# The triangular solves of the RWKV operands issued on VectorE in 30 parts a stage

## The chip, the core and the metric

The kernel runs on one core of a Trainium2 chip. The metric is the device time of one launch in microseconds. An execution's own time is its span, from the first to the last instruction of the program, and what lies around it.

## The reference, cut to what matters

One layer of a hybrid backbone, run over 256 context tokens and 2048 latent tokens, width 1024. One input projection feeds three token mixers: mLSTM (6 heads x 64), RWKV-7 (6 heads x 64) and RG-LRU (256 channels). Their outputs are gated, joined and go through one output projection. The mixers run in both directions.

The change touches RWKV-7. The reference is a scan over tokens, for each head and direction:

```python
def rwkv_step(S, inp):
    r, w, kh, b, kt, v = inp
    Sk = jnp.einsum('bhvk,bhk->bhv', S, kh)
    S = S * w[:, :, None, :] - Sk[..., None] * b[:, :, None, :] + v[..., None] * kt[:, :, None, :]
    return S, jnp.einsum('bhvk,bhk->bhv', S, r)
```

The kernel takes 64 tokens at a time (a chunk). Within a chunk the state products depend on one another through a strictly lower triangular 64x64 matrix, so each chunk needs the inverse of a unit triangular matrix. The kernel inverts its two 32x32 diagonal blocks by substitution and gets the third block by two matrix products.

## The kernel before, in words

The program is written by generators under a small planner (class `Flow`). The planner keeps a clock of its own, `F.now`, that grows with the estimated time of the matmuls it has issued. Each generator issues instructions and yields either a number of ns after which it may go on or an event. Of the generators that may go on the one with the lowest rank goes first; rank 9, the input projection (`projector`), is the filler and is taken when no other is ready, or when TensorE's estimated activity is low. TensorE executes in exactly this written order. The other engines' queues are put in order by a list scheduler from the written order and its own estimates. Every engine executes its queue in order.

The stages, with their times in the profile: inputs, gates and shifts (to about 640 us), `derive` (640 to 1056), `mlstm` (1056 to 1378), `chains` with the output projection (1378 to the end). The projection of 34 column groups runs beside the first three; its tiles are called `pp_` and the group (`pp_rz`, `pp_mo`, `pp_mz` are the last ones). Its very last group may only start after `mlstm`.

`derive` makes the RWKV operands. It has 54 blocks of 256 tokens and one direction, for a pair of heads each, in seven stages (one of 6 blocks, six of 8). `block()` does a block: four matmuls into `pw`, then ScalarE and VectorE in turn up to the tile `KB` (L955 to L972 are VectorE's seven or so instructions), and stores. A worker, one of three, then waits, multiplies `KB` into `pt` on TensorE (16 short matmul records), and copies its 32x32 parts into `DG` and `OF`. When a stage's blocks are through, `derive`'s own loop transposes `DG` into `W` (L1049), masks it on GpSimd (L1050, L1052) and solves: for j from 1 to 30 a product into `tmp` (L1058) and an addition into `W` (L1060), each of (31 - j) x j elements a partition. The two depend on each other and on the step before. `finish` waits, transposes `W` twice into `XT` (L1030, L1031), and starts `merge`: products `pY` and `pX` on TensorE and the store of `XT`. `W` has two buffers, and stage k takes its one when `finish` of stage k - 2 has read it. The last stage's `merge` ends `derive`; the memory of `derive` is then given to `mlstm`.

`mlstm` takes three head pairs. For each it first makes state changes for 18 chunks (`pk` are TensorE's transpositions, `pd` its products, L1261 the state recurrence on VectorE), then the outputs for 18 chunks with three workers (`pm`, `pn` on TensorE, L1301 to L1321 on VectorE). A head pair's states are made while the one before it gives its outputs.

Of the kernel before, what the change touches and what calls it, by code (L numbers as in the profile page):

```python
# [13 lines left out]
ALU = mybir.AluOpType  # L14
# [297 lines left out]
def side(X, ctx):  # L312
# [31 lines left out]
    with tc.tile_pool(name="dv", bufs=1, side="right") as dv:  # L344
        yield from derive(X, dv)
# [487 lines left out]
def derive(X, dv):  # L833
    nc, vec, hv, CH, F = X["nc"], X["vec"], X["hv"], X["CH"], X["F"]
# [62 lines left out]
    def merge(sid, XT, g, end):  # L897

        o = OF[sid]
        hs = [(slice(64 * h, 64 * h + 32), slice(64 * h + 32, 64 * h + 64)) for h in range(2)]  # L900
        yield 7000.0
        pY = X["ps"].tile([128, 16, 32], F32, tag="b", name=f"pY{sid}{g}")
        for l in range(16):
            for a, b in hs:
                F.mm(pY[b, l], o[a, g + l], XT[a, g + l, 32:64])
            if l % 4 == 3:
                yield 0.0
        for a, b in hs:
            nc.scalar.activation(o[b, g:g + 16], pY[b], AF.Copy, scale=-1.0)
        yield 3000.0  # L910
        pX = X["ps"].tile([128, 16, 32], F32, tag="b", name=f"pX{sid}{g}")
        for l in range(16):
            for a, b in hs:
                F.mm(pX[a, l], o[b, g + l], XT[b, g + l, 32:64])
            if l % 4 == 3:
                yield 0.0
        for a, b in hs:
            nc.scalar.activation(XT[a, g:g + 16, 32:64], pX[a], AF.Copy)
        end[0] -= 1
        if end[0]:  # L920
            return
        yield 1000.0
        for p, d, li, nch, lane in stages[sid]:
            for h in range(2):
                r = slice(64 * h, 64 * h + 64)
                nc.sync.dma_start(CH[p, d][r, li:li + nch, 64 + 192 * h:128 + 192 * h], XT[r, lane:lane + nch])
        F.fire(merged[sid])
# [94 lines left out]

    def finish(sid, W):

        yield 40500.0
        if sid and merged[sid - 1].t is None:
            yield merged[sid - 1]
        XT = dv.tile([128, 32, 64], F32, tag="XT", name=f"XT{sid}")
        with X["tc"].high_priority(offset=300):
            nc.vector.transpose(XT[:, :, 0:32].rearrange("p l t -> p t l"), W)  # L1030
            nc.vector.transpose(XT[:, :, 32:64].rearrange("p l s -> p s l"), W.rearrange("p t s -> p s t"))  # L1031
            for h in range(2):
                r = slice(64 * h + 32, 64 * h + 64)
                nc.vector.tensor_copy(XT[r, :, 32:64], XT[r, :, 0:32])
                nc.gpsimd.memset(XT[r, :, 0:32], 0.0)
        F.fire(read[sid])
        end = [2]
        for g in (0, 16):
            F.spawn(merge(sid, XT, g, end), 2)


    for sid, segs in enumerate(stages):
        if full[sid].t is None or full[sid].t > F.now:
            yield full[sid]
        if sid > 1 and read[sid - 2].t is None:
            yield read[sid - 2]
        W = dv.tile([128, 32, 32], F32, tag="W", name=f"W{sid}", bufs=2)
        with X["tc"].high_priority(offset=300):
            nc.vector.transpose(W, DG[sid].rearrange("p l t -> p t l"))  # L1049
        nc.gpsimd.affine_select(out=W, in_=W, pattern=[[1, 32], [-1, 32]], base=0, channel_multiplier=0,  # L1050
                                compare_op=ALU.is_gt, fill=0.0)
        nc.gpsimd.memset(W.rearrange("p a b -> p (a b)")[:, 0:1024:33], 1.0)  # L1052
        F.fire(taken[sid])
        tmp = dv.tile([128, 256], F32, tag="tmp", name=f"tmp{sid}")
        for j in range(1, 31):
            m = 31 - j
            tv = tmp[:, 0:m * j].rearrange("p (a b) -> p a b", a=m)
            nc.gpsimd.tensor_tensor(out=tv, in0=W[:, j + 1:32, j:j + 1].to_broadcast([128, m, j]),  # L1058
                                    in1=W[:, j:j + 1, 0:j].to_broadcast([128, m, j]), op=ALU.mult)
            nc.gpsimd.tensor_tensor(out=W[:, j + 1:32, 0:j], in0=W[:, j + 1:32, 0:j], in1=tv, op=ALU.add)  # L1060
        F.spawn(finish(sid, W), 2)
    yield merged[-1]

# [907 lines left out]
```

## Time and profile before

| | |
|---|---|
| median of 3 runs | 2062.82 us (2059.71 to 2068.17) |
| profiled execution | 2059.59 us, span 2057.9 us |
| TensorE (PE) busy | 1801.6 us, 88% |
| VectorE (DVE) busy | 1367.0 us, 66% |
| ScalarE (ACT) busy | 977.6 us, 48% |
| GpSimd (POOL) busy | 795.0 us, 39% |
| mean granted TensorE clock | 0.933 |

The shares are means over stages that differ much: GpSimd is busy four fifths of the time while it solves and hardly anywhere else before that. PEld is TensorE's load of weights, which overlaps PE. The rows below are in us except where they say ns; a row's last part is the engine's idle time just before such instructions and what ended it.

### The profile page before, as it was taken

The numbers are of one execution on the slowest core, as the hardware profiler recorded it, in microseconds if no ns is written. First come the engines' busy times: TensorE is split into PE (matmuls) and PEld (weight loads), VectorE is DVE, ScalarE is ACT, GpSimd is POOL, SyncE is SP. The second block draws the span as 40 slices with busy tenths as digits, with TensorE's granted clock in tenths as the row PEclk, the third lists the DMA queues.
The fourth block names the chain that finished last, engine by engine and source line by source line (L and its number), as shares of the span: only waits on it lengthen the run. The fifth ranks groups of instructions, "written<-read, shape, count | busy, mean of one in ns | idle before, by whom it ended". The sixth has DMA issues, their size and how long they took to land. (4 is left out here: it accounts for less than half of the span.)

```text
span 2057.9 us, 46221 instructions
## 1 busy us (share of the span) xinstructions
PE 1801.6 (88%) x16648; PEld 1201.0 (58%) x16778; DVE 1367.0 (66%) x3271; ACT 977.6 (48%) x2634; POOL 795.0 (39%) x1200
## 2 busy tenths in 40 slices
PE   5899999999999878788899798878778788999996
PEld 3555655656666556555566565555555556777774
DVE  3747366777643898998324766647885576777774
ACT  5732446565434667776242545542332233444442
POOL 0210011112110688888722444342653232444442
PEclk9899999999999988889999899989888999999997
DMA  7343344564548778887254666645986545576662
GB/s 284 118 142 90 126 123 133 153 168 148 132 127 247 215 207 223 225 214 176 80 154 135 188 171 170 171 118 154 292 268 193 164 136 149 163 196 203 197 190 72
DMA packets 353370, 350.60 MB, mean 170 GB/s; under 512 B 109554, under 2 KB 294978, under 8 KB 350728
## 3 DMA queue, kind: packets, MB, share of 16 engines
q1 hardware_dynamic: 353142, 347.65, 59.2%
q8 instruction: 133, 2.18, 0.5%
q14 instruction: 95, 0.78, 0.1%
HBM read 211.18 MB, written 136.37 MB: 169 GB/s over the span
## 5 line engine op out<-in xcount | busy, mean ns | idle before, releaser
L1635 POOL TENSOR_SCALAR sd<-cg,Dall 128x128 f32<-128x128 f32 x210 | 135.8, 654 | 267.1 <-DVE cg L1659 164.0
L1659 DVE SCALAR_TENSOR_TENSOR cg<-cq,Dall,sd 64x64 f32<-64x64 f32 x408 | 114.5, 281 | 46.4 <-PE cq L168 36.6
L1060 POOL TENSOR_TENSOR W<-W,tmp 128x30 f32<-128x30 f32 (+14 forms) x210 | 139.0, 662 | 16.1
L1058 POOL TENSOR_TENSOR tmp<-W 128x30 f32<-128x30 f32 (+14 forms) x210 | 133.0, 633 | 15.9
L168 PE MATMUL cq<-cg,bt 128*64 128x64 f32 x840 | 68.5, 246 | 49.7 <-DVE cg L1644 44.6
L1283 ACT ACTIVATE nb<-nb,aT 128x128 f32<-128x128 f32 x216 | 71.6, 393 | 82.5 <-DMA nb<-nm_d 72.4
L168 PE MATMUL cq<-cg 128*64 128x64 f32 x1728 | 92.9, 230 | 8.2 <-DVE cg L1659 8.2
L168 PEld LDWEIGHTS cq<-cg,bt 128*64 128x64 f32 x840 | 44.1, 142 | 84.9 <-DVE cg L1644 54.8
L168 PE MATMUL ga<-cg 64*64 64x128 f32 (+1 forms) x864 | 76.9, 270 | 16.9 <-DMA cg<-ch 16.9
L1630 ACT ACTIVATE q<-cq 128x64 f32<-128x64 f32 x216 | 45.5, 223 | 95.7 <-PE cq L168 92.3
L1592 DVE TENSOR_TENSOR cg<-gb,rmask 64x256 f32<-64x256 f32 x108 | 44.7, 413 | 66.3 <-PE gb L168 61.1
L168 PEld LDWEIGHTS cq<-cg 128*64 128x64 f32 x1728 | 72.9, 141 | 24.3 <-issue 9.5
L168 PE MATMUL pz<-owhi,zhi 128*128 128x512 f32 x180 | 82.1, 456 | 4.5 <-ACT zhi L1822 4.5
L1598 ACT ACTIVATE bt<-ga 128x256 f32<-128x256 f32 x108 | 41.3, 383 | 87.0 <-DVE G L1595 83.4
L168 PE MATMUL pt<-KB 64*64 64x64 f32 x864 | 41.9, 244 | 45.7 <-DVE KB L972 45.6
L1284 POOL TENSOR_SCALAR_AFFINE_SELECT nb<-nb 128x256 f32<-128x256 f32 x108 | 44.8, 421 | 93.0 <-ACT nb L1283 63.6
L168 PE MATMUL gb<-cg 64*64 64x128 f32 (+1 forms) x864 | 75.7, 270 | 0.9 <-DMA cg<-ch 0.9
L168 PE MATMUL pz<-owhi,zlo 128*128 128x512 f32 x180 | 73.5, 409 | 3.3 <-DVE zlo L1823 3.3
L168 PE MATMUL pz<-owlo,zhi 128*128 128x512 f32 x180 | 72.9, 405 | 0.0
L168 PEld LDWEIGHTS ga<-cg 64*64 64x64 f32 x864 | 48.2, 142 | 41.9 <-issue 27.9
L168 PE MATMUL cq<-q,cg 128*64 128x64 f32 x864 | 59.4, 236 | 9.9 <-ACT q L1630 9.9
L168 PE MATMUL pp_v<-hhi,whi_v 128*128 128x512 f32 (+1 forms) x120 | 67.4, 562 | 0.3 <-ACT whi_v L514 0.3
(511 smaller groups left out, 6180.0 us busy)
## 6 DMA issues: line engine op xcount, KB each, us to landing
cg<-ch SPq DMA_DIRECT2D x216, 192.0 KB
wa<-wa SPq DMA_DIRECT2D x54, 256.0 KB
z<-z SPq DMA_DIRECT2D x27, 512.0 KB
ch<-KB SPq DMA_DIRECT2D x108, 128.0 KB
ch<-KB SPq DMA_DIRECT2D x54, 256.0 KB
nb<-nm_d SPq DMA_DIRECT2D x108, 128.0 KB
lr<-L SPq DMA_DIRECT2D x16, 768.0 KB
lL<-lr SPq DMA_DIRECT2D x16, 768.0 KB
```

The source lines that it names most:

```text
L168: self.nc.tensor.matmul(out, lhsT, rhs, start=start, stop=stop, **kw)
L1058: nc.gpsimd.tensor_tensor(out=tv, in0=W[:, j + 1:32, j:j + 1].to_broadcast([128, m, j]), in1=W[:, j:j + 1, 0:j].to_broadcast([128, m, j]), ...
L1060: nc.gpsimd.tensor_tensor(out=W[:, j + 1:32, 0:j], in0=W[:, j + 1:32, 0:j], in1=tv, op=ALU.add)
L1283: nc.scalar.activation(nb[:, d, j], nb[:, d, j], AF.Exp, bias=aT[:, c, d, 2 * p + j:2 * p + j + 1])
L1284: nc.gpsimd.affine_select(out=nb[:, d], in_=nb[:, d], pattern=[[0, 2], [1 - 2 * d, 128]], base=0, channel_multiplier=-1 + 2 * d, compare_o ...
L1592: nc.vector.tensor_tensor(out=cg[o, :, RK[h]], in0=src[o], in1=mask[o, d].rearrange("p a c -> p (a c)")[:, None].to_broadcast([64, 2, 128] ...
L1598: nc.scalar.activation(bt, ga[:, 1], AF.Copy)
L1630: nc.scalar.activation(q, qk, AF.Copy, scale=-1.0)
L1635: nc.gpsimd.tensor_scalar(sd, cg.rearrange("p (n c) -> p n c", c=64)[:, 0::9], Dk, None, op0=ALU.mult)
L1659: nc.vector.scalar_tensor_tensor(out=nxt[h][b], in0=ps[b], scalar=Dk[b], in1=sd[b, 1 - h], op0=ALU.mult, op1=ALU.add)
```

## The change

The 60 instructions of a stage's solve are issued on VectorE instead of GpSimd. After each of the 30 steps the loop yields for 800 ns of the planner's clock, so that blocks and filler are written in between; before, the 60 instructions were written in one piece. `finish` waits for 6 us of that clock instead of 40.5.

```diff
     def finish(sid, W):
 
-        yield 40500.0
+        yield 6000.0
         if sid and merged[sid - 1].t is None:
             yield merged[sid - 1]
         XT = dv.tile([128, 32, 64], F32, tag="XT", name=f"XT{sid}")
...
         for j in range(1, 31):
             m = 31 - j
             tv = tmp[:, 0:m * j].rearrange("p (a b) -> p a b", a=m)
-            nc.gpsimd.tensor_tensor(out=tv, in0=W[:, j + 1:32, j:j + 1].to_broadcast([128, m, j]),
+            nc.vector.tensor_tensor(out=tv, in0=W[:, j + 1:32, j:j + 1].to_broadcast([128, m, j]),
                                     in1=W[:, j:j + 1, 0:j].to_broadcast([128, m, j]), op=ALU.mult)
-            nc.gpsimd.tensor_tensor(out=W[:, j + 1:32, 0:j], in0=W[:, j + 1:32, 0:j], in1=tv, op=ALU.add)
+            nc.vector.tensor_tensor(out=W[:, j + 1:32, 0:j], in0=W[:, j + 1:32, 0:j], in1=tv, op=ALU.add)
+
+            yield 800.0
         F.spawn(finish(sid, W), 2)
```

VectorE's queue in `derive`, at one block of the second stage (`KB_0_7681`; `cs` and `E` are its decay factors, `z` its loaded operands). Before:

```order
L959 TENSOR_SCALAR KB_0_7681_6152<-KB_0_7681_6152,rab 128x4x64
L955 TENSOR_SCALAR cs_0_7681_6155<-KB_0_7681_6152 128x256
L965 TENSOR_TENSOR KB_0_7681_6152<-KB_0_7681_6152,z_0_768_5887 128x4x128
L956 SCALAR_TENSOR_TENSOR cs_0_7681_6155<-sm,cs_0_7681_6155 128x256
L967 TENSOR_TENSOR KB_0_7681_6152<-E_5316,z_0_768_5887 128x4x64
L969 TENSOR_TENSOR KB_0_7681_6152<-E_5316,z_0_768_5887 128x4x64
L972 TENSOR_TENSOR KB_0_7681_6152<-cs_0_7681_6155,KB_0_7681_6152 128x4x128
L955 TENSOR_SCALAR cs_0_10240_6259<-KB_0_10240_6256 128x256
L959 TENSOR_SCALAR KB_0_10240_6256<-KB_0_10240_6256,rab 128x4x64
```

The block's seven instructions follow each other, and the next block's come right behind them.

The same block now (`W` and `tmp` are those of the first stage's solve):

```order
L959 TENSOR_SCALAR KB_0_7681_6108<-KB_0_7681_6108,rab 128x4x64
L972 TENSOR_TENSOR KB_0_7680_6068<-cs_0_7680_6071,KB_0_7680_6068 128x4x128
L955 TENSOR_SCALAR cs_0_7681_6111<-KB_0_7681_6108 128x256
L1058 TENSOR_TENSOR tmp_5941<-W_5937 128x168
L965 TENSOR_TENSOR KB_0_7681_6108<-KB_0_7681_6108,z_0_768_5887 128x4x128
L956 SCALAR_TENSOR_TENSOR cs_0_7681_6111<-sm,cs_0_7681_6111 128x256
L1060 TENSOR_TENSOR W_5937<-W_5937,tmp_5941 128x24x7
L1058 TENSOR_TENSOR tmp_5941<-W_5937 128x184
L967 TENSOR_TENSOR KB_0_7681_6108<-E_5316,z_0_768_5887 128x4x64
L969 TENSOR_TENSOR KB_0_7681_6108<-E_5316,z_0_768_5887 128x4x64
L1060 TENSOR_TENSOR W_5937<-W_5937,tmp_5941 128x23x8
L972 TENSOR_TENSOR KB_0_7681_6108<-cs_0_7681_6111,KB_0_7681_6108 128x4x128
```

Between the seven instructions of the block stand instructions of the solve, and where no block is ready they follow each other.

TensorE's queue near the end of `mlstm`, in the outputs of the third head pair (`pm` and `pn` are its products, `pp_mo` is projection). Before:

```order
L168 MATMUL pm_14544<-kq_14278 128x128
L168 MATMUL pm_14544<-dl_12404,kq_14278 128x130
L168 MATMUL pm_14550<-kq_14278 128x128
L168 MATMUL pm_14550<-dl_12404,kq_14278 128x130
L168 MATMUL pm_14555<-kq_14278 128x128
L168 MATMUL pm_14555<-dl_12404,kq_14278 128x130
L168 MATMUL pn_14560<-v_10445,nb_14384 64x65 x8
L168 MATMUL pp_mo_3_14490<-hhi,whi_mo_13783 128x512
L168 MATMUL pp_mo_3_14490<-hhi,wlo_mo_13784 128x512
L168 LDWEIGHTS w_mo_13785
L168 MATMUL pp_mo_3_14490<-hlo,w_mo_13785 128x512
L168 MATMUL pp_mo_3_14490<-hhi,whi_mo_13783 128x512
```

Pieces of six projection matmuls stand between the products.

The same part now:

```order
L168 MATMUL pm_14580<-kq_14361 128x128
L168 MATMUL pm_14580<-dl_12810,kq_14361 128x130
L168 MATMUL pm_14585<-kq_14361 128x128
L168 MATMUL pm_14585<-dl_12810,kq_14361 128x130
L175 MATMUL hT_14590<-ident,H 128x128 x4
L168 MATMUL pm_14599<-kq_14361 128x128
L168 MATMUL pm_14599<-dl_12810,kq_14361 128x130
L168 MATMUL pm_14604<-kq_14361 128x128
L168 MATMUL pm_14604<-dl_12810,kq_14361 128x130
L168 MATMUL pn_14609<-v_10847,nb_14455 64x65 x8
L168 MATMUL pn_14625<-v_10849,nb_14476 64x65 x8
L168 MATMUL pn_14641<-v_10851,nb_14497 64x65 x8
```

The projection that stood between the products isn't there any more. It stands in `derive`: TensorE's order holds 1284 projection matmuls between the first `pw` and the first `pk`, 990 before. In the first half of `mlstm` as much of it stands in the same places, and from the first matmul of the chains on TensorE's order is the same as before.

## Rows read from the trace of the kernel before

**Rows 1.** Windows of five stages: us, busy us of each engine, PEclk, DMA, GB/s.

```profile
680.00:975.00 295.00, 239.42 (x2754) 165.41 (x2784) 272.36 (x373) 210.81 (x652) 252.90 (x364) 0.85 0.79 207
975.00:1056.00 81.00, 72.32 (x790) 47.53 (x797) 22.30 (x26) 21.69 (x38) 46.28 (x101) 0.94 0.37 97
1056.00:1205.00 149.00, 135.50 (x1028) 87.55 (x1043) 80.40 (x296) 64.17 (x203) 59.10 (x142) 0.94 0.61 168
1205.00:1292.00 87.00, 72.97 (x695) 49.88 (x702) 56.45 (x229) 44.75 (x137) 43.19 (x98) 0.94 0.63 171
1292.00:1378.00 86.00, 72.44 (x637) 47.86 (x643) 50.43 (x187) 42.53 (x100) 34.10 (x79) 0.96 0.48 138
```

**Rows 2.** Groups of GpSimd, 680 to 1026 us: busy us, mean ns, idle before.

```profile
L1060 POOL TENSOR_TENSOR W<-W,tmp 128x30 f32<-128x30 f32 (+14 forms) x210 | 139.0, 662 | 16.1
L1058 POOL TENSOR_TENSOR tmp<-W 128x30 f32<-128x30 f32 (+14 forms) x210 | 133.0, 633 | 15.9
```

**Rows 3.** Waits of GpSimd, 684 to 1026 us: us, times, longest.

```profile
POOL W L1050 <- DVE W L1049: 7.3, 5, 2.4
```

**Rows 4.** Single lines and tiles: ns min/median/max, first and last start, forms.

```profile
L1058 POOL TENSOR_TENSOR tmp<-W x210: 237/610/1117, 683.6 to 1024.5; 128x30 f32<-128x30 f32 x7, 128x84 f32<-128x84 f32 x7, 128x130 f32<-128x130 f32 x7, 128x168 f32<-128x168 f32 x7
...
L1031 DVE STREAM_TRANSPOSE XT<-W x7: 2062/2092/2223, 731.7 to 1026.9; 128x1024 f32<-128x1024 f32 x7
...
L168 PE MATMUL pt<-KB x864: 218/218/366, 652.3 to 969.1; 64*64 64x64 f32 x173
...
L175 PE MATMUL pk<-ident,vk x108: 272/273/475, 1056.4 to 1264.6; 128*128 128x128 f32 x108
```

**Rows 5.** Groups of VectorE before the solves, 640 to 680 us.

```profile
L965 DVE TENSOR_TENSOR KB<-KB,z 128x512 f32<-128x512 f32 x7 | 4.8, 679 | 0.1
...
L972 DVE TENSOR_TENSOR KB<-cs,KB 128x512 f32<-128x512 f32 x6 | 4.0, 685 | 0.0
...
L967 DVE TENSOR_TENSOR KB<-E,z 128x256 f32<-128x256 f32 x7 | 3.0, 423 | 2.1 <-ACT E L957 2.1
...
L955 DVE TENSOR_SCALAR cs<-KB 128x256 f32<-128x256 f32 x8 | 2.3, 289 | 8.4 <-ACT KB L950 8.4
```

**Rows 6.** Groups of VectorE beside the solves, 684 to 980 us.

```profile
L972 DVE TENSOR_TENSOR KB<-cs,KB 128x512 f32<-128x512 f32 x48 | 44.2, 925 | 3.2 <-ACT cs L958 3.2
...
L965 DVE TENSOR_TENSOR KB<-KB,z 128x512 f32<-128x512 f32 x47 | 42.6, 910 | 0.0
...
L1030 DVE STREAM_TRANSPOSE XT<-W 128x1024 f32<-128x1024 f32 x5 | 9.7, 1950 | 0.0
```

**Rows 7.** Timeline of VectorE from 202 us: start, us, instruction.

```profile
202.37 0.16 DVE L79 TENSOR_TENSOR lpz<-lpz,ly 128x4 f32<-128x4 f32 x1
202.57 0.16 DVE L81 TENSOR_TENSOR lpw<-lpz 128x4 f32<-128x4 f32 x1
```

**Rows 8.** Group of VectorE, 138.5 to 141 us.

```profile
L84 DVE SCALAR_TENSOR_TENSOR mlpq<-mlpq,mlpw 128x216 f32<-128x216 f32 x6 | 2.3, 383 | 0.2
```

**Rows 9.** Timelines of VectorE from 645 us and of TensorE from 687.5 us.

```profile
647.26 0.42 DVE L967 TENSOR_TENSOR KB<-E,z 128x256 f32<-128x256 f32 x1
...
647.60 0.42 DVE L971 TENSOR_TENSOR KB<-E,z 128x256 f32<-128x256 f32 x1
...
687.83 1.12 PE L168 MATMUL pt<-KB 64*64 64x64 f32 x16
```

**Rows 10.** Waits of TensorE, 680 to 1056 us: us, times, longest.

```profile
PE pt L168 <- DVE KB L972: 43.5, 20, 5.7
PE pY L168 <- DVE XT L1031: 14.1, 3, 5.8
```

**Rows 11.** Waits of VectorE and two tiles' busy time, 1205 to 1378 us.

```profile
DVE H L1321 <- POOL t L1316: 16.3, 18, 2.8
...
1205.00:1378.00 173.00, 45.23 (x162) 20.69 (x116) 4.44 (x8) 0.95 0.56 154
...
1205.00:1378.00 173.00, 37.69 (x152) 19.64 (x104) 3.84 (x6) 3.35 (x6) 0.95 0.56 154
```

## The prediction

> **What bounds the kernel now.** I read the windows by stage first, then the stage that the change touches, engine by engine, then the stage behind it. The operands of the RWKV chains are built from about 640 to 1056 us, the mLSTM group runs from 1056 to 1378, the chains from 1378 to the end [rows 1]. TensorE is busy for 135.5 of the 149 us from 1056 to 1205, but only for 239 of the 295 from 680 to 975, at a granted clock of 0.85, a mix of its two levels (1.2 and 2.4 GHz). In those 295 us VectorE is busy for 272 and GpSimd for 253 [rows 1]. Two things set the pace there. GpSimd runs seven solves of 60 instructions, 272 us in all [rows 2], and between the first solve and the last it waits only 7.3 us for the transposition that starts a solve [rows 3]: the solves stand end to end from 683.6 to 1025 us [rows 4]. And VectorE is slow: its instructions with two inputs in SBUF took 679 to 685 ns (128x512) before the solves began [rows 5] and 910 to 925 ns beside them [rows 6], while the stream transposition, with one input, stayed at 1950. TensorE waits 43.5 us for VectorE's last product of a block and 14.1 us for the transposed solves [rows 10].
>
> This is where a rule of the Trainium skill bears on the case. SBUF — State Buffer, section Who interferes with whom, says that a VectorE instruction with two SBUF inputs contends with a GpSimd instruction that reads SBUF, and that one with a single input outside the two-port modes does not. The trace agrees on both kinds (685 against 925, and 1950). Were the longer times VectorE's own, the sum below would be some 70 us higher.
>
> **The change part by part.**
>
> *Solves.* GpSimd loses 420 instructions, VectorE gets them. The trace has none of them on VectorE, so I price them by nearest rows. A dependent 128x4 product starts 0.20 us after the one before it and lasts 0.16 [rows 7]; a dependent 128x216 one lasts 383 ns [rows 8]. That is 159 ns plus 1.04 ns per element. The loop has 4,960 elements per operation and stage, so 69,440 in all: 420 x 0.159 + 69,440 x 0.00104 = 139 us. An instruction that doesn't need the one before it starts some 83 ns before that one's end (0.34 us apart, 0.42 long) [rows 9]; one that does starts 35 ns behind it. In the new order 237 of the 420 are followed by a dependent: 139 + 237 x 0.035 - 183 x 0.083 = 132 us of VectorE's queue. Bounds: all dependent, 154 us; at the element price of the one-input L955 (289 ns for 256 elements, 0.51 ns each, [rows 5]) 95, which no instruction with two inputs shows. I take 132; the bounds move the sum by +22 and -37.
>
> *What VectorE gets back.* The other 399 instructions that stand in its new order from the first transposition (680 us) to the last, at the undisturbed means of [rows 5] and with the same overlap, are 209 us. Together 341 us, against 349 (680 to 1029) that the same stretch took before. So VectorE has room only if nothing makes it wait.
>
> *The blocks (first half of that stretch).* By the new order the 46 blocks from the eighth one on are 271 us of VectorE work; TensorE's between the same places is 236: some 670 projection matmuls at 0.26 us (82.9 us for 314, [rows 11]) and 62 us of the blocks' and merges' own, since more projection is put between the blocks. Both queues are in order and each waits for the other about once per three blocks (three workers). Taking per bunch of three the longer of the two gives 305 us; VectorE alone 271. Before, from the eighth block's product (687.8) to the last one's (969.1) [rows 4, 9], it was 281. I take 296, nearer the upper end since both engines are then over 80% busy: **+15** (bounds -10 to +46, the latter with the 22 us that VectorE is idle from 680 to 975 [rows 1] added again).
>
> *The tail.* Before, after the last block GpSimd does one solve and the last transposition ends at 1029, 60 us behind 969. Now VectorE still has 67 us of queue there: the rest of one solve, a whole one, and six transpositions of 2 us, with nothing to share it. With some waits for evacuations 75: **+15** (bounds +7 to +25). What is late next is TensorE's projection, put in front of the last products: it fits in those 75 us. From the transposition to the first mLSTM transposition (1056.4) both orders hold the same instructions, so 27 us stay 27.
>
> *The filler.* Between the first block and the first mLSTM instruction TensorE's order holds 990 projection matmuls before, 1284 now. The first half of the mLSTM stretch (1056 to 1205) holds 378 in both. The second half (1205 to 1378) holds 330 before and 36 now. So in that half TensorE loses 83 us of its 145 busy ones (45.2 + 37.7 of all projection there) [rows 1, 11], and what counts is how much of the 173 us goes with them. VectorE is busy there for 107 and waits 16.3 for GpSimd's products [rows 1, 11]; that is 9.4 us of work for each of six rounds in the 87 us up to 1292, and 8.4 for each of six in the 86 after it. Three workers take turns, so a round can't come down to VectorE's work alone: I expect 2.5 us less for each of the first six, and 5 us for the rest. **-20** (bounds 0 and -44; the latter is VectorE's 100 us of mLSTM work plus 29 us in which it now stands still at the turn to the last group and at the end). TensorE that idles is granted less clock (0.85 where it was busy 81%, [rows 1]), which speaks for the smaller gain. From the chains' first matmul on TensorE's order is the same: 0.
>
> *Sum:* 15 + 15 - 20 = +10 us. The profiled execution took 2059.6 us (span 2057.9), the median of the runs is 2062.8; the same difference on the median gives 2072.8, so 2073.
>
> **The rivals.**
>
> *VectorE's queue stays full* (ends on the other side). Place: the blocks from 688 to 969. If the workers ride far enough ahead that TensorE never makes VectorE wait, that stretch takes 271, -10 instead of +15, and the tail +7 for +15: -3, with -20 behind it -23, 2040 us. For it: VectorE is the one that is behind all through this stretch, idle for 22 us only. Against: TensorE's part is 236 of the 271, and pieces of 10 to 17 us of projection stand between the bunches. It decides once the last transposition ends less than 10 us later than 1029. The Trainium skill leans this way: GPSIMD Engine Reference, section Engine selection, wants elementwise products on VectorE, GpSimd being about half as fast with two inputs. My 139 us against 272 say the same of one instruction; the rule says nothing of an engine that is full.
>
> *The queues lock.* Every block's step stands behind solve instructions, and its product, first in TensorE's queue, holds the projection behind it. Then the bunches cost 305 and VectorE's 22 us of idle time come again (+46), the tail +25, and the rounds of the mLSTM gain 10 only: +61, 2124. For it: TensorE waits 43.5 us for the same product already. Against: most solve instructions are only 0.2 to 0.4 us long and nothing but VectorE feeds them.
>
> *The filler pays back all.* The second mLSTM half falls to its VectorE floor, -44: 15 + 15 - 44 = -14, 2049. For it: TensorE has 62 us left there. Against: between the groups the state recurrence (34 steps in a row) can't be hurried.
>
> That the change does nothing isn't likely to be told from these: the solve leaves GpSimd for certain.
>
> **How the numbers follow.** Forecast 0.45, with its own range 2054 to 2092; full queue 0.20; locked queues 0.22; pay-back 0.13. About 10 us, 0.5%, is what a measurement of this kernel can tell from no change. The forecast lies at that edge: half of its chance is slower, most of the rest the same. Slower: 0.23 + 0.21 = 0.44. Faster: 0.05 + 0.15 + 0.09 = 0.29. The same: 0.27. The range leaves out a tenth on each side: 2034 to 2120.
>
> **What would show it.** In the changed profile: 128x512 products near 690 ns all through the stretch (else the contention was not what made them long); solve instructions at 0.2 to 0.4 us, 139 us in sum; the last transposition near 1059 (by 1035: the full queue; past 1085: the locked queues); TensorE's waits for the block's product under 60 us; the first mLSTM transposition near 1086; about 300 us from there to the first chain matmul instead of 322. I am wrong if a solve instruction costs twice its price, or if the mLSTM stretch keeps its 322 us.

## The result and the profile after

| | before | after |
|---|---|---|
| median (4 runs each, same chip) | 2063.03 us (2059.71 to 2068.17) | 2093.28 us (2088.21 to 2097.73) |
| profiled execution, span | 2059.59, 2057.9 us | 2096.72, 2095.0 us |
| mean granted TensorE clock | 0.933 | 0.919 |

The ratio is 1.0144, 95% interval 1.0108 to 1.0179: 30 us slower, where +10 was forecast. The profiled pair lies 37 us apart, 7 more than the medians; the balance below is that of this pair. In the changed kernel the lines behind the solve stand two numbers higher (L1301 is L1303).

The same stages, cut at the same events (eighth and last block's product, first mLSTM transposition, turn to the second mLSTM half, first chain matmul). First two windows of before, cut so; the columns are those of [rows 1].

```profile
689.00:969.00 280.00, 229.64 (x2684) 158.74 (x2717) 260.51 (x359) 201.31 (x623) 241.50 (x344) 0.85 0.80 209
969.00:1056.00 87.00, 78.32 (x826) 51.08 (x830) 25.74 (x28) 25.95 (x50) 51.58 (x110) 0.94 0.41 103
```

Then the windows of after, the second mLSTM half in two pieces as in [rows 1].

```profile
686.00:1006.00 320.00, 262.51 (x2806) 177.72 (x2803) 291.92 (x701) 205.43 (x639) 19.84 (x20) 0.87 0.72 195
1006.00:1104.00 98.00, 98.00 (x1048) 62.36 (x1045) 52.44 (x114) 28.77 (x54) 7.42 (x22) 1.00 0.40 104
1104.00:1257.00 153.00, 135.74 (x1039) 89.02 (x1037) 80.93 (x296) 63.79 (x202) 59.86 (x142) 0.92 0.59 163
1257.00:1343.00 86.00, 56.10 (x584) 41.95 (x582) 58.61 (x229) 45.68 (x137) 46.37 (x105) 0.73 0.58 156
1343.00:1416.00 73.00, 48.00 (x473) 37.78 (x471) 46.28 (x175) 32.14 (x79) 30.69 (x73) 0.69 0.42 115
```

Read them as a balance. Blocks: 280 to 320 us, **+39** between the products. Between the last product and the mLSTM: 87 to 98, **+11**, and TensorE, idle for 9 us there before, is busy in all 98. First mLSTM half (149 in [rows 1]): 153, **+4.5**. Second half (87 and 86): 159, **-14**. Everything behind the first chain matmul: the same within a microsecond. The sum is +40; less the 2.4 us by which the eighth block came earlier and 0.7 us less in the chains, that is the 37 us between the spans.

The groups of VectorE between 678 and 1060 us (solve) and between 684 and 980 (products) answer to [rows 2, 6]: line, engine, operation, count, busy us, mean ns, idle before.

```profile
L1058 DVE TENSOR_TENSOR tmp<-W 128x30 f32<-128x30 f32 (+14 forms) x210 | 70.6, 336 | 4.0
L1060 DVE TENSOR_TENSOR W<-W,tmp 128x30 f32<-128x30 f32 (+14 forms) x210 | 69.9, 333 | 4.7
...
L972 DVE TENSOR_TENSOR KB<-cs,KB 128x512 f32<-128x512 f32 x45 | 30.7, 685 | 2.0 <-ACT cs L958 2.0
L965 DVE TENSOR_TENSOR KB<-KB,z 128x512 f32<-128x512 f32 x45 | 30.6, 679 | 0.2
```

The solve costs VectorE 140.5 us (139 forecast), and the products are back at the lengths of [rows 5]: 685 instead of 925 ns. The price of the instructions was right; the loss doesn't lie in their length.

TensorE's waits from 680 to 1104 us answer to [rows 10]: us, times, longest.

```profile
PE pt L168 <- DVE KB L972: 31.0, 10, 7.6
PE pY L168 <- DVE tmp L1058: 20.6, 3, 10.9
PE pY L168 <- DVE XT L1031: 10.2, 1, 10.2
```

Single lines and tiles (ns, first and last start) answer to [rows 4].

```profile
L1058 DVE TENSOR_TENSOR tmp<-W x210: 163/349/1423, 684.2 to 1052.5; 128x30 f32<-128x30 f32 x7, 128x84 f32<-128x84 f32 x7, 128x130 f32<-128x130 f32 x7, 128x168 f32<-128x168 f32 x7
...
L1031 DVE STREAM_TRANSPOSE XT<-W x7: 2076/2089/2230, 751.9 to 1057.7; 128x1024 f32<-128x1024 f32 x7
...
L168 PE MATMUL pt<-KB x864: 218/218/366, 650.3 to 1005.9; 64*64 64x64 f32 x173
...
L175 PE MATMUL pk<-ident,vk x108: 272/273/476, 1103.9 to 1328.6; 128*128 128x128 f32 x108
```

TensorE now stands for 31 us before pY, the first product of a stage's merge, for 14.1 before. The fifth stage shows how. VectorE's first and last transposition of that stage, before:

```profile
875.44 1.99 DVE L1049 STREAM_TRANSPOSE W<-DG 128x1024 f32<-128x1024 f32 x1
...
942.47 2.08 DVE L1031 STREAM_TRANSPOSE XT<-W 128x1024 f32<-128x1024 f32 x1
```

and after, with the fourth stage's last transposition, the first and the last instruction of the fifth solve and the last block's product L972 between them:

```profile
888.71 2.00 DVE L1049 STREAM_TRANSPOSE W<-DG 128x1024 f32<-128x1024 f32 x1
...
920.26 2.10 DVE L1031 STREAM_TRANSPOSE XT<-W 128x1024 f32<-128x1024 f32 x1
922.23 0.20 DVE L1058 TENSOR_TENSOR tmp<-W 128x30 f32<-128x30 f32 x1
...
983.12 0.68 DVE L972 TENSOR_TENSOR KB<-cs,KB 128x512 f32<-128x512 f32 x1
...
985.79 0.19 DVE L1060 TENSOR_TENSOR W<-W,tmp 128x30 f32<-128x30 f32 x1
...
987.85 2.08 DVE L1031 STREAM_TRANSPOSE XT<-W 128x1024 f32<-128x1024 f32 x1
```

What TensorE did then (its wait, and what ended it, in brackets):

```profile
978.80 1.12 PE L168 MATMUL pt<-KB 64*64 64x64 f32 x16 [7.63 <-DVE KB L972]
990.07 2.34 PE L168 MATMUL pY<-XT,OF 32*32 32x32 f32 x80 [7.26 <-DVE tmp L1058]
...
1003.19 0.68 PE L168 MATMUL pt<-KB 64*64 64x64 f32 x16
1005.39 0.68 PE L168 MATMUL pt<-KB 64*64 64x64 f32 x16
```

Each solve instruction is half as long as on GpSimd, and yet the solve comes back later: 99 us from one transposition to the other instead of 67. The fifth solve begins only when the fourth stage's last transposition is done, 34 us after its own stage's first one, and its 20 us of instructions then take 64, with VectorE's work for the blocks and the projection between them. So the seven solves stand end to end on VectorE, from 684.2 to 1053 us, as they did on GpSimd from 683.6 to 1025 [rows 4].

TensorE meets pY at 982.8, stands until 990, and the last block's product, whose input VectorE had finished at 983.8, runs at 1005.4 behind pY and the projection. pY isn't earlier in TensorE's order than it was: in the first five stages it begins after 18, 28, 36, 44 and 52 blocks' products, before after 17, 26, 34, 41 and 50. It is early only against the solve.

### The profile page after: what moved, and what is told of

The parts are those of the page before. It is cut to its first block, busy times and chain, and to the rows that moved or that the text cites. A ratio compares the mean times of both kernels' runs of the same rounds, so it can differ in the third digit from the quotient of the medians.

```text
span 2095.0 us, 46346 instructions
## 1 busy us (share of the span) xinstructions
PE 1812.6 (87%) x16778; PEld 1214.9 (58%) x16778; DVE 1422.0 (68%) x3691; ACT 975.1 (47%) x2634; POOL 522.3 (25%) x780
## 5 line engine op out<-in xcount | busy, mean ns | idle before, releaser
L1035 POOL MEMSET XT<- 32x1024 f32 x14 | 16.1, 1153 | 235.1 <-DVE XT L1034 92.9
L1058 DVE TENSOR_TENSOR tmp<-W 128x30 f32<-128x30 f32 (+14 forms) x210 | 70.6, 336 | 4.0
L1060 DVE TENSOR_TENSOR W<-W,tmp 128x30 f32<-128x30 f32 (+14 forms) x210 | 69.9, 333 | 4.7
L168 PE MATMUL pn<-v,nb 128*64 128x65 f32 x864 | 49.4, 276 | 25.0 <-DVE nb L1303 11.1
```

Of the source, the lines that this page charges most:

```text
L168: self.nc.tensor.matmul(out, lhsT, rhs, start=start, stop=stop, **kw)
L1058: nc.vector.tensor_tensor(out=tv, in0=W[:, j + 1:32, j:j + 1].to_broadcast([128, m, j]), in1=W[:, j:j + 1, 0:j].to_broadcast([128, m, j]), ...
L1060: nc.vector.tensor_tensor(out=W[:, j + 1:32, 0:j], in0=W[:, j + 1:32, 0:j], in1=tv, op=ALU.add)
```

## The experiments

Two theories. *Order*: the planned waits of the change (30 times 800 ns, 6 us instead of 40.5) put 294 projection matmuls more into the derivation and bring pY to the head of TensorE's queue before the solve is back, and that is what costs, whichever engine solves. *Load*: VectorE is too full with 139 us more. The comparisons are with runs of before on the same chip: 2059.58 us (e1 to e4), 2063.61 (e5 to e8), 2064.12 (e9 to e11).

**e1, the engine alone.** From the changed kernel:

```diff
-        yield 6000.0
+        yield 40500.0
...
-            yield 800.0
```

> The solve on VectorE, but all 60 instructions of a stage in one piece and the merge 40.5 planned us behind them, so TensorE's order is that of the kernel before, matmul for matmul (990 projection matmuls from the first block to the first mLSTM transposition, 330 in the second mLSTM half). Theory A (what costs is the order: the 294 projection matmuls that came into the derivation and the early pY; the engine's price is about paid by the end of the contention): the last block's product at 975 to 990 us instead of 1005.9, the first mLSTM transposition near 1060 to 1075 instead of 1103.9, the mLSTM stretch 322 us as before, 2065 to 2080 in all. Theory B (VectorE is over full with 139 us of solve, whatever the order): the first transposition at 1095 to 1110 and, with no filler gone from the mLSTM half, 322 us behind it: 2100 to 2115. A lump of 19 us on VectorE seven times could make TensorE wait 7 x 5 to 10 us for the blocks in either.

Measured: 2082.26, ratio 1.0103 (1.0062 to 1.0145). Blocks 312 us (+32 against before), first mLSTM transposition 1081.7, no theory's number. The solve is written in one piece, but on VectorE it is no lump of 19 us: the queue holds the blocks' instructions between its own, and the fifth solve takes 56 us from its first instruction to its last.

```profile
916.60 0.17 DVE L1058 TENSOR_TENSOR tmp<-W 128x30 f32<-128x30 f32 x1
...
972.91 0.19 DVE L1060 TENSOR_TENSOR W<-W,tmp 128x30 f32<-128x30 f32 x1
```

With TensorE's order of before, each solve, and what it delays, shows as a stop at pY, one in each of the seven stages:

```profile
PE pY L168 <- DVE tmp L1058: 43.7, 4, 16.5
PE pY L168 <- DVE XT L1031: 30.4, 3, 15.3
PE pt L168 <- DVE KB L972: 18.1, 8, 6.9
```

**e2, the order alone.** From the changed kernel:

```diff
-            nc.vector.tensor_tensor(out=tv, in0=W[:, j + 1:32, j:j + 1].to_broadcast([128, m, j]),
+            nc.gpsimd.tensor_tensor(out=tv, in0=W[:, j + 1:32, j:j + 1].to_broadcast([128, m, j]),
...
-            nc.vector.tensor_tensor(out=W[:, j + 1:32, 0:j], in0=W[:, j + 1:32, 0:j], in1=tv, op=ALU.add)
+            nc.gpsimd.tensor_tensor(out=W[:, j + 1:32, 0:j], in0=W[:, j + 1:32, 0:j], in1=tv, op=ALU.add)
```

> The solve stays on GpSimd, with the 30 parts and the 6 us of the change: TensorE's order is that of the changed kernel, matmul for matmul; the engine alone is undone. Theory A (the order is what costs): as slow as the changed kernel or slower, since pY now stands early and the solve behind it takes 39 us instead of 20 on its engine: first mLSTM transposition 1110 to 1130, then about 310 us as in the changed kernel, 2100 to 2120. Theory B (VectorE's load is what costs, the order is harmless): the first transposition near 1056 to 1070, 2045 to 2060, below the kernel before.

Measured: 2104.13, 1.0213 (1.0173 to 1.0253), the first transposition at 1113.4: *order*, as expected. But not by way of pY: TensorE's waits of this kernel hold none for it, and more for the blocks' products, which VectorE makes in 902 ns again beside GpSimd's solve. With no stop at pY left to blame, what costs here is the projection that came in: TensorE is busy for 269 of 331 us in the blocks, before for 230 of 280.

```profile
PE pt L168 <- DVE KB L972: 60.2, 16, 9.1
```

VectorE's product in the same kernel, 690 to 950 us:

```profile
L972 DVE TENSOR_TENSOR KB<-cs,KB 128x512 f32<-128x512 f32 x38 | 34.0, 902 | 2.6 <-ACT cs L958 2.6
```

**e3, shorter planned parts.** From the changed kernel:

```diff
-        yield 6000.0
+        yield 12000.0
...
-            yield 800.0
+            yield 200.0
```

> The changed kernel with 200 instead of 800 planned ns behind each of the 30 parts and 12 instead of 6 us to the merge. The planner then puts 1014 projection matmuls into the derivation (changed kernel 1284, before 990) and leaves 300 in the second mLSTM half (36, 330); pY stands one block later. VectorE does the same 420 instructions in parts. Theory A: the tail shrinks back (54 projection matmuls fewer than the changed kernel between the last block and the last merge, and 168 fewer among the blocks, 0.26 us each): first mLSTM transposition 1060 to 1080 instead of 1103.9, the half behind it 173 us as before; 2065 to 2085. Theory B (VectorE's 139 us are the cost): transposition stays at 1095 to 1105 and the filler's gain of 14 us is lost as well: 2100 to 2115.

Measured: 2082.51, 1.0115 (1.0080 to 1.0149), at the upper end of *order*: first transposition 1071.2, but 330 us from there to the chains (changed kernel 312), and 55.5 us of stops at pY. Less projection makes TensorE arrive earlier and wait. And pY stands a block later only in the first stage; in the next four it begins after 25, 34, 43 and 51 blocks, one to three earlier than in the changed kernel.

**e4, pY later.** From the changed kernel:

```diff
-        yield 6000.0
+        yield 25000.0
```

> The changed kernel with 25 instead of 6 planned us between the last part and the merge: TensorE meets each pY three to four blocks later in its order (22 blocks instead of 18 at the first), the projection stays where the change has it (1308 matmuls in the derivation, 36 in the second mLSTM half). If TensorE's stops at pY among the blocks are what lengthens them (31 us of waits for the solve and the transposition, and VectorE's products lying ready meanwhile): the last block's product 12 to 25 us earlier than 1005.9, the tail as long as before, 2070 to 2085. If VectorE's own load sets the blocks, or the projection between them: the waits for pY turn into waits for the block's product, the last product within 5 us of 1005.9, and 2088 to 2100.

Measured: 2075.80, 1.0078 (1.0054 to 1.0102): 16 us above before, where the changed kernel is 30 above. The last block's product is at 989.6, 16 us earlier. Of 31 us of stops at pY 9 are left, and 10 us of waiting at a block's product came in. Only the first stage's pY stands later by whole blocks (22 for 18); the others begin after 28, 36, 44 and 52 as in the changed kernel, with their last parts up to two blocks later. Between the eighth and the last product it is 15 us. So the stops at pY cost the changed kernel about 15 us there; the tail took 102 (98 in the changed kernel), TensorE busy throughout.

```profile
PE pt L168 <- DVE KB L972: 31.0, 8, 10.8
PE pt L168 <- DVE tmp L1058: 9.9, 1, 9.9
PE pY L168 <- DVE W L1060: 8.8, 1, 8.8
```

**e5, no solve in the order of the change.** The two instructions of the loop are left out, the 30 planned parts stay:

```diff
-            nc.vector.tensor_tensor(out=tv, ...
-            nc.vector.tensor_tensor(out=W[:, j + 1:32, 0:j], ...
```

> The changed kernel with the 420 solve instructions left out and everything else, the 30 planned parts too, in its place: TensorE's order is that of the changed kernel, matmul for matmul. It leaves the triangular inverse out, so its time only prices the solve. Theory A+B (in the blocks VectorE's 292 busy us of 320 are the bound, in the tail TensorE's are): VectorE falls to about 175 busy us in the blocks and TensorE's own 262 take over: the last block's product at 950 to 965 instead of 1005.9; the tail stays 95 to 100 us, since TensorE is busy for all of it; the first mLSTM transposition 1048 to 1062, 2040 to 2055 in all. Rival (TensorE's order with its early pY and its projection is the bound by itself, VectorE only follows): the last product stays at 985 or later, 2070 to 2090.

Measured: 2084.18 (2 runs), 1.0105 (1.0079 to 1.0131). The rival's numbers came: without any solve the kernel is still 21 us slower than before with one. VectorE is down to 204 busy us of 305 in the blocks, and TensorE, with the same 262 busy us and 40 of waits for the blocks' products, takes 305. No stop at pY is left, so it is the projection that binds here, not pY. With all 420 instructions on VectorE and pY moved, e4 took the same 305 us in nearly the same order. The tail is TensorE's alone.

```profile
687.00:992.00 305.00, 262.26 (x2767) 177.92 (x2796) 203.77 (x373) 207.62 (x639) 20.23 (x20) 0.88 0.75 204
992.00:1090.00 98.00, 97.99 (x1040) 62.34 (x1049) 24.92 (x28) 28.77 (x54) 7.40 (x22) 1.00 0.39 101
```

Its waits of TensorE from 678 to 1090 us:

```profile
PE pt L168 <- DVE KB L972: 40.3, 14, 8.4
```

**e6, both mends.** e4's edit, and in `side`:

```diff
+        F.share(0.45, True)
         yield from derive(X, dv)
+        F.share(0.0)
```

> The two mends together: pY late as in the kernel with 25 planned us (first at 22 blocks), and the projection held back while the operands are derived (a share of 0.45 of the planned time), so that the derivation holds 936 projection matmuls (before 990, changed kernel 1284), the second mLSTM half 408 (330, 36), the chains 108 (84, 84). VectorE does all 420 instructions. If stops at pY and the extra projection are the whole loss of the changed kernel: blocks 285 to 292 us (VectorE is busy for 280 of them), tail 82 to 86, the first mLSTM transposition at 1055 to 1065, then 322 to 330: 2058 to 2072, within noise of before. If VectorE's load stretches the blocks whatever TensorE does: blocks near 299 to 305 again, 2078 to 2090.

Measured: 2149.80, 1.0422 (1.0401 to 1.0443), a plain miss. Blocks 302, with 37 us of stops at pY again; first transposition 1079.4; then the second mLSTM half takes 202 us with 408 projection matmuls, and the last part of the chains 31 us more, where TensorE waits 39 us for the output's inputs (8 in the changed kernel). Holding back the projection changes the order behind the derivation too; as a test of the sum of both mends this run says little.

**e7, the last solve on VectorE, its merge planned earlier.** From the kernel before:

```diff
-        yield 40500.0
+        yield 20000.0 if sid == 6 else 40500.0
...
+        eng = nc.vector if sid == 6 else nc.gpsimd
```

(and `eng` in both instructions)

> The kernel before with one solve of the seven on VectorE, the last, where VectorE is busy for only 26 of the 87 us between the last block and the mLSTM (its merge planned after 20 us instead of 40.5). TensorE's order up to the last block is that of before; behind it stand 60 projection matmuls fewer, which go to the mLSTM half and the chains (366 and 114 instead of 330 and 84). Theory (an engine change pays where its new engine stands idle): the last transposition at 1000 to 1010 instead of 1026.9, the first mLSTM transposition 1038 to 1045 instead of 1056.4, the mLSTM stretch 322 to 328: 2043 to 2055. Rival (TensorE, busy for 78 of those 87 us, only changes what it waits for, and the 60 matmuls cost the same elsewhere): 2057 to 2063.

Measured: 2070.25, 1.0042 (1.0019 to 1.0065), slower, above both ranges. The first mLSTM transposition came at 1050.5, 6 us earlier, but the second half took 190 us instead of 173 with 36 matmuls more. These are 9 us at 0.26; where the other 8 come from this run doesn't show.

**e8, a filler that computes nothing.** In the projector of the changed kernel, where only the last tile is left and it waits for the mLSTM:

```diff
-        if not free and not shift and X["mlstm"].t is None:
-            yield X["mlstm"]
+        if not free and not shift:
+            while X["mlstm"].t is None:
+                pd = X["ps"].tile([128, 512], F32, tag="b", name="pdummy")
+                for k in range(24):
+                    F.mm(pd, hhi[:, k % NK, 0:128], hhi[:, k % NK, 0:512], start=(k == 0), stop=(k == 23))
+                    if k % 6 == 5:
+                        yield 0.0
```

> The changed kernel; where its projection runs dry in the mLSTM group, TensorE gets 336 matmuls of the same shape (128x512) that nobody reads, put in by the same rule as the projection (before had 330 of the projection there, the changed kernel 36; 30 of these move behind, into the chains). No other engine gets work from them. If the low granted clock of 0.7 in that half keeps back what the missing filler gave: the mLSTM's own matmuls fall from 276 to about 240 ns, the clock is 0.9 or more there, and the half stays within 5 us of the changed kernel's 159 although TensorE does 80 us more: 2088 to 2096 in all. If the clock costs nothing there and the filler itself is what lengthens the half (TensorE in order, the state's matmuls behind it): the half goes back to 170 to 175, 2103 to 2112.

Measured: 2118.79, 1.0271 (1.0247 to 1.0295). The second mLSTM half of e8 by windows, all instructions:

```profile
1265.00:1435.00 170.00, 150.90 (x1360) 115.60 (x1359) 100.69 (x403) 77.14 (x215) 77.73 (x179) 0.97 0.49 129
```

In the same stretch the products pn alone (PE, PEld, DVE):

```profile
1265.00:1435.00 170.00, 25.24 (x576) 21.19 (x576) 14.89 (x36) 0.97 0.49 129
```

and in the changed kernel:

```profile
1257.00:1416.00 159.00, 36.48 (x576) 30.55 (x576) 14.59 (x36) 0.71 0.51 137
```

The granted clock came back (0.97 for 0.71) and the 576 products took 25 instead of 36 us; still the half grew by 10.5 us. So the lower clock did hold these products back, but a filler that restores it costs more than it gives: the theory's claim on the clock holds, its consequence falls. Of the 25 us between the spans of the two, another 6.4 lie in the chains, where the 30 matmuls went; 5.4 lie before the eighth block's product and 2.6 in the first mLSTM half, where the two programs hold the same instructions.

**e9, no solve in the order of before.** The kernel before without the two instructions of the loop (as e5).

> The kernel before with the 420 solve instructions left out: TensorE's order is that of before, matmul for matmul. It leaves the triangular inverse out; its time says what the solve, on whichever engine, can cost in that order. Theory C (in the blocks two bounds lie close together, VectorE's work and TensorE's in-order queue with its waits for each block's product; taking the solve away meets the other): TensorE's own 230 busy us plus 35 us of waits for the product remain: blocks 262 to 270 instead of 280.5, the tail 80 to 82 (TensorE is busy for 79 of it), the first mLSTM transposition near 1030 to 1040, 2030 to 2042. Rival (the solve is what paces the blocks in the order of before): blocks 235 to 245, the transposition near 1005 to 1015, 2005 to 2018.

Measured: 2018.86, 0.9794 (0.9763 to 0.9825). Blocks and tail:

```profile
687.00:951.00 264.00, 228.29 (x2683) 158.38 (x2714) 195.78 (x360) 202.62 (x627) 19.21 (x20) 0.85 0.83 225
951.00:1027.00 76.00, 74.47 (x829) 48.08 (x833) 25.16 (x28) 24.67 (x47) 7.40 (x22) 1.00 0.42 108
```

The blocks at 264 are theory C's; the tail of 76 and the first transposition at 1027.3 lie a little below its range, and the median lies at the edge of the rival's time (the profiled span, 2025.9, between the two). The solve paces the blocks of before less than the rival had it. VectorE has 196 busy us in place of 260.51 with the same instructions: 65 us of what it did before went with GpSimd's solve. The Trainium skill (SBUF — State Buffer, section Who interferes with whom) says that a VectorE instruction with two SBUF inputs contends with a GpSimd one that reads SBUF. The trace agrees: the product L972 takes 685 ns here, 925 before [rows 6]. Yet in the changed order the same step (e5 against e2) was worth 22 us, no more.

**e10, the last solve on VectorE, nothing else.** e7 without its first edit; TensorE's order is that of before.

> The kernel before with the last of the seven solves on VectorE and nothing else: TensorE's order is that of before, matmul for matmul (the kernel with the last solve tried already had 60 projection matmuls fewer there). In the tail GpSimd's 39 us become 20 on VectorE, busy for 26 of 87 us there; TensorE's 79 busy us are next. Expected: the last transposition 1008 to 1015 instead of 1026.9, the first mLSTM transposition 1050 to 1052 instead of 1056.4, nothing behind it changed: 4 to 6 us less than before, 2053 to 2057 against 2060. Rival (TensorE's order decides already: last pY stands behind 210 projection matmuls): no more than 2 us less.

Measured: 2057.08 (12 runs), 0.9979 (0.9962 to 0.9995): 7 us by the medians, 4 by the profiled spans, for the 4 to 6 expected; the interval reaches from 1 to 8. It is the only version with the solve in it that is faster than before. The tail:

```profile
970.00:1051.00 81.00, 77.05 (x832) 50.34 (x840) 44.09 (x88) 25.00 (x48) 20.07 (x48) 0.96 0.44 112
```

The last transposition and the first mLSTM one (last and first start):

```profile
L1031 DVE STREAM_TRANSPOSE XT<-W x7: 2084/2099/2252, 729.3 to 1022.4; 128x1024 f32<-128x1024 f32 x7
...
L175 PE MATMUL pk<-ident,vk x108: 272/273/447, 1051.1 to 1262.6; 128*128 128x128 f32 x108
```

TensorE, busy for 77 of 81 us, stops the gain there. The last transposition came only 4.5 us earlier, not 12 to 19: the last solve stands on VectorE behind the sixth stage's transposition, which waits for GpSimd's sixth solve, and begins at 989.68. And it takes 31 us there instead of 20, with the projection's instructions L657 and L516 between its own.

```profile
985.93 1.90 DVE L1030 STREAM_TRANSPOSE XT<-W 128x1024 f32<-128x1024 f32 x1 [4.55 <-POOL W L1061]
...
989.68 0.17 DVE L1059 TENSOR_TENSOR tmp<-W 128x30 f32<-128x30 f32 x1
```

**e11, every second solve on VectorE.** As e7, with `sid % 2` in place of `sid == 6`.

> The kernel before with three of the seven solves on VectorE (the second, fourth and sixth), each in one piece, its merge planned after 20 us instead of 40.5; 996 projection matmuls in the derivation (before 990). GpSimd's solves no longer stand end to end, and about half of the blocks run without contention. Theory C: VectorE's 260 busy us in the blocks lose about 40 of contention and gain 59 of solve: about 280 again, blocks 282 to 295, 2060 to 2075. Rival (GpSimd's chain of seven solves is what sets the blocks' pace): blocks 255 to 268, 2035 to 2050.

Measured: 2086.65, 1.0115 (1.0068 to 1.0162). VectorE's 262 busy us are below the 280 expected, and the blocks still take 303: TensorE stands 50.5 us before pY, for the three stages of VectorE, three times up to 18.4.

```profile
PE pY L168 <- DVE XT L1031: 50.5, 3, 18.4
PE pt L168 <- DVE KB L972: 38.1, 14, 5.9
```

**Together** (median us; ratio to before on the same chip):

| TensorE's order | no solve | solve on GpSimd | solve on VectorE |
|---|---|---|---|
| of before | 2018.86 (0.9794) | before (1) | 2082.26 (1.0103), written in one piece |
| of the change | 2084.18 (1.0105) | 2104.13 (1.0213) | 2093.28 (1.0144) |

The order costs 65 us where nobody solves (2084.18 - 2018.86), about 44 on GpSimd (0.0213 of 2064), some 8 on VectorE. The solve costs 43 to 45 us on GpSimd and some 64 on VectorE in the order of before (1 and 1.0103 against 0.9794), and 22 and 8 in the order of the change. The two 8s lie inside the intervals of the runs. The costs don't add: the two queues take turns at being late, and once TensorE's order alone needs 305 us for the blocks, VectorE's solve fits almost under it.

## Why the prediction was right in its sign and short in its size

*Solves, contention:* right. 140.5 us against 139, 685 ns against 690. The last transposition ended at 1059.8, forecast 1059, but that is luck: the last block's product came 22 us later than the forecast's sum has it, and VectorE needed 21 us less behind it (54 for 75).

*The blocks* are the step that failed: +39 for the +15 taken, inside its bounds of -10 to +46. Two things in it were wrong, and the experiments separate them.
- TensorE's part was put at 236 us; it is 262. Of that sum the projection came out: 174 us for some 670 matmuls, measured 178 for 732, added up over their tiles. The term that was mis-sized is the blocks' and merges' own work, put at 62 us: 84 are left for it. Before already had 229.64 busy us with 204 matmuls fewer, so 236 could have been seen to be too low. With the waits for products TensorE needs 305 with no solve at all (e5), against 264 in the order of before (e9).
- The bunch model knew only one wait, for the block's product. It was under 60 us as forecast (31.0), but the stops at pY came beside it, 31 us for 14.1. The prediction priced the solve by its instructions; what TensorE meets is the time from the stage's first transposition to its last, which grew from 67 to 99 us in the fifth stage. Much of that is the order's: with no solve it is 82 us in the order of the change (e5) and 61 in that of before (e9). e4, where pY is moved and the projection hardly, takes 15 of the 39 us back.

In TensorE's own balance 33 of the 40 us between the two windows are busy time and 7 are idle.

*The tail:* the length came out (75 + 27 = 102 forecast, 98 measured), its parts and its bound did not. The prediction let TensorE's projection "fit in those 75 us"; TensorE is busy for all 98, the same 98 without any solve (e5). The 27 us from the end of the last transposition to the first mLSTM one became 44, and the 75 before them 54.

*The filler:* -20 was taken, -14 came in the second half, and the first half gave 4.5 back, though both orders hold the same matmuls there: from the first transposition to the chains 312 us, forecast 300. The granted clock fell from 0.95 to 0.71, as the argument for the smaller gain had it, and e8 shows the products pn 11 us longer by it. TensorE's busy time there fell by 41 us (145 to 104), not by the 83 of the prediction. No run came near the -44 of "The filler pays back all".

*Rivals.* The outcome (+30 by the medians, +37 by the profiled pair) lies between the forecast and "The queues lock" (+61). That rival had the blocks almost right (+46; 39 came, with VectorE idle for 28 us of the 320) and the mLSTM (10; 9.7 came), though TensorE's head is held by the late solve rather than by the product alone; its tail (+25; 11 came) and its mark, a last transposition past 1085, are not there. "VectorE's queue stays full" fell by its own mark: the last transposition came 31 us after 1026.9, not less than 10.

Not settled: how much of e3's rest is the place of pY and how much the projection, since every edit of the planned waits also moved the projection. In e1 too VectorE's queue mixes the solve with the blocks, so it isn't the writing in parts alone that makes it long; an order of VectorE's queue that brings the solve back sooner was not tried.

## What to carry to other kernels

Moving work to a faster engine shortens the instructions, not the time until the result is back: on an in-order queue that is full, count the stretch from the first to the last instruction of the moved work, and look at which other queue has that result at its head. When the edit also changes planned waits, take the new order apart from the new engine: run each alone, and both orders without the moved work. Move the part whose new engine is idle there (here the last solve, 0.2% faster, at the edge of what the runs can tell) and leave the rest.

## What the runs showed of the hardware

- VectorE's 128x512 product with two inputs in SBUF (L972) follows GpSimd's share of work: 902 ns with GpSimd solving throughout (e2), 805 with four of the seven solves on it (e11), 685 with none (e9).
- Small dependent products on VectorE cost what two rows of before had suggested: 336 and 333 ns mean over forms of 30 to 240 elements.
- TensorE's granted clock in the second mLSTM half was 0.95 when it was busy for 145 of 173 us, 0.71 when busy for 104 of 159, and 0.97 when useless matmuls filled it. The Trainium skill asks for a TensorE that is kept busy (TensorE: Matmul & The Clock Gate, section Why this matters for your kernels). The clock agrees; the time here does not: 170 us with the filler, 159 without.
